# Holding a layer's projections close behind the attention that they are woven with, and moving one gate tile to another buffer tag

## The chip, the cores and the metric

The kernel runs on one core of one Trainium2 chip. The metric is the device time of one execution in microseconds. Before the change it is 1248.79 us, the median of three runs (1248.63 to 1249.88).

## The reference

Two transformer layers work on 512 latent tokens (an 8 x 64 grid) and 256 context tokens, D = 1024, heads of 64. Each layer computes, in float32:

```
hx = rmsnorm(x) * (1 + scale) + shift          # shift, scale, gate from c @ ada_w + ada_b
px = hx @ w_in                                 # 1024 x 4608, split into q, k, v of A, B, C and a gate path
ya = A: global attention, 8 heads, 2 kv heads, q and k normalised and rotated
yb = B: neighbourhood attention, 8 heads, 8 x 16 window, learned bias
yc = C: window of +-128 tokens, 8 heads, 2 kv heads, a sink logit
x  = x + gate * ((concat(ya, yb, yc) * silu(px_gate)) @ w_out)
```

All three kinds of attention also read the 256 context keys. In the first layer the context tokens are queries too and are carried on; in the second they are only keys. A final RMSNorm gives the output.

## The kernel before, in words

**Precision.** Every large product is taken in three: each operand is split into a high and a low float32r part (hi x hi, hi x lo, lo x hi). So a projection of one 512-column bank is 8 k-tiles x 3 = 24 matmuls, and each weight tile is split first, by ScalarE (line 172, the high part) and VectorE or GpSimd (line 175, the low part).

**Stages.** For each layer, `mixers` runs the projections and the attention, then a stage of eight output blocks (`block`) multiplies by `w_out`. In front of the first layer stands the normalisation of x.

**Projections.** `proj_f` (matmuls on line 237) gives features x tokens: one bank of 512 latent columns and, where the context is wanted, one of 256. `proj_t` (line 258) gives tokens x features: two token tiles to a bank, 48 matmuls of 256 columns. Both take PSUM banks of tag pj, of which there are two, and hand a finished bank to a callback `done`, traced at high priority. The callbacks split Q, K and V, rotate (A's pairs 1 to 3 on GpSimd, lines 576 to 657), and compute the gates: `g_silu` (lines 634 and 635) for A and B, `c_g` (lines 779 and 780) for C.

**Attention.** A *pair* is two heads of one kind: B0 to B3, A0 to A3, C0 to C3. For each unit of a pair `scores` multiplies Q and K (line 881 for A, 924 and 926 for C, 979 and 981 for B, 846 for the context queries) and takes maximum and exponential. `values` transposes the probabilities (lines 901, 953, 1006, 864), splits them (line 553 on ScalarE and 798 on VectorE) and multiplies by V (`pv`, line 804). The values of one unit are zipped with the scores of the next. `finish` divides by the sums, transposes the result (line 1070) and multiplies by the gate; for C that is on GpSimd (lines 1076 and 1078), and the last read of C's gate.

**The weave.** `PLAN` (line 32) lists steps. Each step runs one pair's attention and the projections for later pairs: A0 with C's k, v and pair c0; C0 with a1; A1 with c1; C1 with a2; A2 with c2; C2 with a3; A3 with c3. The four B steps carry B's remaining projections, A's k and v, and a0. `weave` (line 1129) draws from two generators in turn, so that both progress in the same share of their estimated TensorE time. The attention's estimates are 16.5 (A) and 12.5 (B, C), plus 2.7 in layer 0 (lines 1211 and 1212); each `yield` tells how much was just issued. C3, the last, is woven with `head`, which reloads the finished products u (tile uf) and starts the first two output blocks (line 426).

**What sets the order on an engine.** The weave gives only the order in which instructions are traced, and with it their priority. The framework then schedules them by a timeline that it estimates when the program is built (line 1369): on each engine it takes the ready instruction of the highest priority, so an instruction traced later may be placed earlier when those ahead of it are not ready. The order on each engine is fixed from then on. `after` (line 96) adds a dependency without a semaphore: an order on one engine, and no wait between engines.

**Buffers.** A tag is a set of equal rooms, and a tile waits until a room is free. Tag gt has three rooms of 768 columns: the gates of A, B and C, and the reloaded uf of the head (line 404). Tag bm has two of 1152 columns: B's bias masks, one for each head (line 1154), and C's mask msk of 896 columns (line 1172), which is loaded once per layer when A0 begins and read until C3's scores. The reloaded u are split into the h tiles that the projections have read.

Of the kernel before, what the change touches and what calls it, by code (L numbers as in the profile page):

```python
# [18 lines left out]
D = 1024  # L19
# [26 lines left out]

CFG = dict(hp=600, hpf=600, pj=2, T=2, O=1, P=5, qt=5, kt=4, vt=4, gt=3, wh=5, ws=3, pt=3, bm=2, tA=1, OT=1, u=1, tl=1, ab="pj", tR=1, map={}, ada=2, h0=300, h1=1000, a0=9, H=2, hr=0, cp="A", cv="A", w0="D", w1="D", w2=(("D", "D"), ("D", "D")), hb="D", ws_="P")

# [12 lines left out]
def body(tc, xT, small, bcast, rpb, adaw, wt, wf, wo, trigA, trigC, mskB, mskC, outT):  # L61
# [153 lines left out]
    def wrap_h(kt):  # L215
        for h in (hh, hl):
            t = h[kt][2]
            nc.scalar.activation(t[:, 0:64], t[:, NT:NT + 64].bitcast(F32), AF.Copy)

    def off_tile(h, t):  # L220

        return h[2][:, t * 128:t * 128 + 128] if t < 4 else cols(h, t * 128, 128)

    def proj_f(l, s, need_ctx, bank, done):

        banks = early.pop(("f", s), None)
        w = None if banks else load_wf(l, s)
        for c0, n in ((0, NT), (NT, NCX)):
            if c0 and not need_ctx:
                continue  # L230
            p = banks.pop(0) if banks else bank()
            i = 0
            for kt in range(KT if w else 0):
                wh, wl = w[kt // 4]
                r = kt % 4
                for a, b in ((wh, hh), (wh, hl), (wl, hh)):
                    nc.tensor.matmul(p[:, 0:n], a[:, r, :], cols(b[kt], c0, n), start=(i == 0), stop=(i == 23))  # L237
# [7 lines left out]
    def proj_t(l, s, tiles, bank, done, tok=None):  # L245

        tok = tok or (lambda h, t: cols(h, t * 128, 128))
        banks = early.pop(("t", s), None)
        w = None if banks else load_wt(l, s)
        for t2 in range(0, tiles, 2):  # L250
            p = banks.pop(0) if banks else bank()
            for t in range(0 if w is None else 2):
                i = 0
                for kt in range(KT):
                    wh, wl = w[kt // 2]
                    r = kt % 2
                    for a, b in ((hh, wh), (hh, wl), (hl, wh)):
                        nc.tensor.matmul(p[:, t * 256:(t + 1) * 256], tok(a[kt], t2 + t), b[:, r, :],  # L258
                                         start=(i == 0), stop=(i == 23))
# [267 lines left out]
def mixers(tc, nc, l, last, p1, ps, const, env):  # L527
    g_ = env
    en = g_["en"]
    (pj, Sbig, psT, psO, half_O, opv, after, ADA, wlo, proj_f, proj_t, ada, ada_load, ident, identr, bc, onesw, mhalf, negsink, udram, dram, hpool, rpb,  # L530
# [243 lines left out]
    def c_g(i, bank):  # L774
        G = newG()

# [16 lines left out]
    def pt_copy(T, n):  # L793
# [5 lines left out]
        return hi, lo  # L799

    def pv(O, v, pt, o, c0, n, first, final):

        for x in range(2):
            a = nc.tensor.matmul(O if c0 is None else O[:, c0:c0 + n], v, pt[x][:, o:o + n], start=first and x == 0,  # L804
                                 stop=final and x == 1, skip_group_check=True)
# [35 lines left out]
    class CtxUnit(Unit):  # L841
        def scores(self):
            S = Sbig[:, 0:512]
            for t in range(2):
                for x in range(2):
                    nc.tensor.matmul(S[:, t * 256:(t + 1) * 256], self.Q[:, NT + t * 128:NT + (t + 1) * 128],
                                     self.K[:, x, NT:NA], start=(t == 0 and x == 0), stop=(x == 1),
                                     skip_group_check=True)
# [11 lines left out]
        def values(self):  # L860
            T = psT()
            for kb in range(2):
                for t in range(2):
                    nc.tensor.transpose(T[:, (2 * kb + t) * 128:(2 * kb + t + 1) * 128],
                                        self.P[:, t * 256 + kb * 128:t * 256 + (kb + 1) * 128], ident)
# [8 lines left out]
    class GlobalUnit(Unit):  # L874
        def scores(self):
            self.P = []
            for i in self.tiles:
                cx, loc = ((512, 0), (768, 1024))[i % 2]
                for c0, c1, o in ((NT, NA, cx), (0, NT, loc)):
                    for x in range(2):  # L880
                        nc.tensor.matmul(Sbig[:, o:o + c1 - c0], self.Q[:, i * 128:(i + 1) * 128],  # L881
                                         self.K[:, x, c0:c1], start=(x == 0), stop=(x == 1), skip_group_check=True)
# [10 lines left out]
        def values(self):  # L893
            O = half_O()
            for k2 in range(0, 6, 2):
                T = psT()
                for k in range(2):
                    for j in range(2):

                        o = ((k2 + k + 2) % 6 if j else k2 + k) * 128  # L900
                        nc.tensor.transpose(T[:, (2 * k + j) * 128:(2 * k + j + 1) * 128], self.P[j][:, o:o + 128],  # L901
                                            ident)
# [9 lines left out]
    class BandUnit(Unit):  # L912
        def scores(self):
# [3 lines left out]
            for pair in ((1, 2), (0, 3)):  # L917
                for i in pair:
# [4 lines left out]
                    for x in range(2):  # L923
                        nc.tensor.matmul(Sbig[:, cx:cx + 256], q, self.K[:, x, NT:NA],
                                         start=(x == 0), stop=(x == 1), skip_group_check=True)
                        nc.tensor.matmul(Sbig[:, loc:loc + nl], q, self.K[:, x, ks[0] * 128:ks[0] * 128 + nl],  # L926
                                         start=(x == 0 and nl > 256), stop=(x == 1), skip_group_check=True)
# [18 lines left out]
        def values(self):  # L946
            O = psO()
            for n, kb in enumerate((4, 5, 0, 1, 2, 3)):
                qs = [i for i in range(4) if kb in self.pos[i]]
                T = psT()  # L950
                for j, i in enumerate(qs):
                    o = self.pos[i][kb]
                    nc.tensor.transpose(T[:, j * 128:(j + 1) * 128], self.P[i][:, o:o + 128], ident)  # L953
                k = len(qs) * 128
# [6 lines left out]
    class NearUnit(Unit):  # L961
# [9 lines left out]
        def scores(self):  # L971
            self.P = {}
            for i in (1, 2, 0, 3):
# [4 lines left out]
                for x in range(2):  # L978
                    a = nc.tensor.matmul(S[:, cx:cx + 256], q, self.K[:, x, NT:NA], start=(x == 0), stop=(x == 1),  # L979
                                         skip_group_check=True)  # L980
                    b = nc.tensor.matmul(S[:, loc:loc + nl], q, self.K[:, x, k0:k0 + nl], start=False,  # L981
                                         stop=(x == 1), skip_group_check=True)
# [16 lines left out]
        def values(self):  # L999
            O = psO()  # L1000
            for n, kb in enumerate((4, 5, 1, 2, 3, 0)):
                qs = [i for i in range(4) if kb in self.PLAN[i][4]]
                T = psT()
                for j, i in enumerate(qs):
                    o = self.PLAN[i][4][kb]
                    nc.tensor.transpose(T[:, j * 128:(j + 1) * 128], self.P[i][:, o:o + 128], ident)  # L1006
                k = len(qs) * 128
# [34 lines left out]
    def finish(c):  # L1042
# [22 lines left out]
        for c0, n in ((0, 4), (4, nq - 4)):  # L1065
# [3 lines left out]
            for t in range(n):  # L1069
                nc.tensor.transpose(T[:, t * 128:(t + 1) * 128],  # L1070
                                    R[:, c0 + t].rearrange("p h f -> p (h f)"), ident)
# [302 lines left out]
```

## Time and profile before

| what | us |
|---|---|
| median of three runs | 1248.79 |
| the profiled execution, its own time | 1248.77 |
| its span, from the first to the last instruction | 1247.0 |
| busy VectorE / ScalarE / GpSimd | 751.5 / 709.7 / 414.5 |

The profile is that of one execution. Busy time of TensorE is that of its matmuls, whose ends are modelled. A row "line engine op out<-in xcount: minimum/median/maximum, first to last" gives durations in ns and the first and last start in us from the span's start. A row of waits gives the waiting instruction, what it waited for, the total, the number and the longest, in us. A row of a stretch gives its bounds and length, each engine's busy time with its number of instructions, the granted TensorE clock, the share of time in which the DMA engines were busy, and GB/s.

In layer 0 the projections and attention run until about 634 us and in layer 1 from about 718 to 1187 us; output blocks follow each.

### The profile page before, as it was taken

The page shows a single profiled execution, that of the slowest core. Times are in us where ns is not written, and L with a number is a line of the kernel's source. Part 1 is how long each engine was busy: PE and PEld are TensorE (multiplying, and loading weights), DVE is VectorE, ACT ScalarE, POOL GpSimd, SP SyncE. Part 2 cuts the span into 40 slices and gives each one's busy share as a digit, 9 for nine tenths or more (in the row PEclk, how much of TensorE's full clock was granted, in tenths as well). Part 3 has the DMA queues.
Part 4 walks back from the last instruction along what each step waited for, and adds up shares of the span by engine and source line. Part 5 has one row for each costly group of instructions (what it writes and reads, how often), then busy time and mean ns, then how long its engine had stood idle before and what let it go on. Part 6 is the DMA issues. An engine that isn't in the chain of part 4 may idle for free.

```text
span 1247.0 us, 21968 instructions
## 1 busy us (share of the span) xinstructions
PE 1177.4 (94%) x8100; PEld 1044.2 (84%) x8100; DVE 751.5 (60%) x1541; ACT 709.7 (57%) x1606; POOL 414.5 (33%) x505
## 2 busy tenths in 40 slices
PE   5999999999999999998899999999999989898996
PEld 3899999898888888886778989989989979777874
DVE  5665666754656647557654864676653465667653
ACT  5454555665655556567644743555665665767651
POOL 2530211353454355534210020201363754634200
PEclk9999999999999999999899999999999999999997
DMA  9442222312244234112245642333222211111251
GB/s 333 158 133 76 91 78 89 113 60 89 86 130 142 81 127 132 47 43 72 77 161 168 187 146 76 94 93 101 87 72 71 70 51 52 43 51 35 85 160 68
DMA packets 59627, 125.55 MB, mean 101 GB/s; under 512 B 7168, under 2 KB 11392, under 8 KB 59520
## 3 DMA queue, kind: packets, MB, share of 16 engines
q1 hardware_dynamic: 53280, 112.48, 28.6%
q10 hardware_dynamic: 6240, 11.67, 2.7%
q8 instruction: 64, 1.05, 0.3%
q14 instruction: 43, 0.35, 0.1%
HBM read 111.41 MB, written 10.09 MB: 97 GB/s over the span
## 4 chain that ended last, share of the span: by engine, by line
PE 77%; DVE 7%; issue 6%; ACT 4%; POOL 2%; DMA 2%; ACTq 0%; SPq 0%; POOLq 0%; DVEq 0%
PE pj L237 18%; PE pj L258 17%; PE Obig L804 8%; PE pj L426 4%; PE Sbig L881 3%; PE T L901 3%; PE T L258 2%; PE Sbig L426 2%; PE T L1006 2%; PE T L953 2%; PE pj L139 2%; PE Sbig L339 1%; PE T L426 1%; PE Sbig L926 1%; PE Sbig L979 1%
## 5 line engine op out<-in xcount | busy, mean ns | idle before, releaser
L798 DVE TENSOR_TENSOR ptl<-T,pth 128x512 fp32r<-128x512 f32 (+2 forms) x312 | 179.6, 590 | 120.3 <-ACT pth L553 118.3
L553 ACT ACTIVATE pth<-T 128x512 fp32r<-128x512 f32 (+2 forms) x312 | 157.1, 519 | 134.9 <-PE T L1006 46.1
L172 ACT ACTIVATE wh<-ws 128x512 fp32r<-128x512 f32 x216 | 133.8, 628 | 116.2 <-PE pj L237 26.8
L258 PE MATMUL pj<-wh,hL 128*128 128x256 f32 x896 | 179.0, 288 | 1.1 <-DVE kt L681 0.9
L237 PE MATMUL pj<-hL,wh 128*128 128x512 f32 x544 | 175.4, 398 | 4.8 <-ACT wh L172 3.0
L804 PE MATMUL Obig<-pth,vt 128*128 128x256 f32 (+2 forms) x432 | 134.9, 321 | 14.3 <-ACT pth L553 8.1
L258 PEld LDWEIGHTS pj<-wh,hL 128*128 128x128 f32 x896 | 143.6, 191 | 5.0 <-issue 2.0
L175 DVE TENSOR_TENSOR wl<-ws,wh 128x512 fp32r<-128x512 f32 x140 | 101.0, 728 | 72.9 <-ACT wh L172 66.5
L804 PE MATMUL Obig<-ptl,vt 128*128 128x256 f32 (+2 forms) x432 | 133.3, 323 | 2.7 <-DVE ptl L798 2.0
L258 PE MATMUL pj<-wl,hL 128*128 128x256 f32 x448 | 128.7, 287 | 0.0
L175 POOL TENSOR_TENSOR wl<-ws,wh 128x512 fp32r<-128x512 f32 x76 | 98.4, 1305 | 89.2 <-ACT wh L172 79.9
L237 PEld LDWEIGHTS pj<-hL,wh 128*128 128x128 f32 x544 | 100.0, 190 | 23.9 <-ACT wh L172 3.5
L237 PE MATMUL pj<-hL,wl 128*128 128x512 f32 x272 | 107.9, 397 | 0.0
L804 PEld LDWEIGHTS Obig<-pth,vt 128*128 128x128 f32 x432 | 82.2, 190 | 26.5 <-ACT pth L553 17.7
L804 PEld LDWEIGHTS Obig<-ptl,vt 128*128 128x128 f32 x432 | 82.3, 191 | 11.9 <-DVE ptl L798 7.0
L1160 POOL TENSOR_TENSOR bm<-wr,bm 128x192 f32<-128x192 f32 (+1 forms) x48 | 38.0, 821 | 153.4 <-DMA bm<-mskB_dram 108.8
L258 PEld LDWEIGHTS pj<-wl,hL 128*128 128x128 f32 x448 | 85.5, 191 | 0.8 <-issue 0.4
L887 DVE TENSOR_REDUCE negm<-Sbig 128x1 f32<-128x768 f32 x64 | 61.0, 954 | 32.3 <-PE Sbig L881 18.6
L935 DVE CUSTOM_DVE_ANT_0 P<-Sbig,msk,negsink 128x640 f32<-128x640 f32 (+1 forms) x64 | 50.9, 815 | 38.6 <-PE Sbig L926 17.2
L815 DVE TENSOR_TENSOR OT<-Obig,otmp 64x512 f32<-64x512 f32 (+1 forms) x88 | 45.0, 511 | 41.2 <-ACT otmp L814 39.8
L237 PE MATMUL pj<-hC,wh 128*128 128x256 f32 x336 | 66.9, 288 | 0.7 <-DVE gt L780 0.5
L992 DVE CUSTOM_DVE_ANT_0 P<-Sbig,bm 128x512 f32<-128x512 f32 (+1 forms) x64 | 41.9, 655 | 41.5 <-PE Sbig L981 28.3
(297 smaller groups left out, 2949.7 us busy)
## 6 DMA issues: line engine op xcount, KB each, us to landing
ada<-adaw_dram SPq DMA_DIRECT2D x48, 512.0 KB, 4.6
ws<-wf_dram SPq DMA_DIRECT2D x72, 256.0 KB, 2.8
ws<-wt_dram SPq DMA_DIRECT2D x72, 256.0 KB, 3.0
ws<-wo_dram SPq DMA_DIRECT2D x72, 256.0 KB, 2.8
bm<-mskB_dram SPq DMA_DIRECT2D x16, 576.0 KB, 4.0
u<-u ACTq DMA_DIRECT2D x9, 384.0 KB, 2.9
uf<-u SPq DMA_DIRECT2D x9, 384.0 KB, 3.0
tB<-tA ACTq DMA_DIRECT2D x40, 64.0 KB, 2.4
```

The source lines that it names most:

```text
L172: nc.scalar.activation(hi, src, AF.Copy)
L175: eng.tensor_sub(lo, src, hi.bitcast(F32))
L237: nc.tensor.matmul(p[:, 0:n], a[:, r, :], cols(b[kt], c0, n), start=(i == 0), stop=(i == 23))
L258: nc.tensor.matmul(p[:, t * 256:(t + 1) * 256], tok(a[kt], t2 + t), b[:, r, :], start=(i == 0), stop=(i == 23))
L426: nc.tensor.matmul(p[:, 0:n], a[:, r, :], ucols(ua[b][ft], c0, n), start=(ft == FT_ORDER[0] and i == 0), stop=(ft == FT_ORDER[-1] and i == 2))
L553: nc.scalar.activation(out, src, AF.Copy)
L798: nc.vector.tensor_sub(lo[:, 0:n], T[:, 0:n], hi[:, 0:n].bitcast(F32))
L804: a = nc.tensor.matmul(O if c0 is None else O[:, c0:c0 + n], v, pt[x][:, o:o + n], start=first and x == 0, stop=final and x == 1, skip_gro ...
L815: nc.vector.tensor_add(OT[64 * h:64 * h + 64, c0:c0 + n], O[0:64, 0:n], tmp[:, 0:n])
L887: nc.vector.tensor_reduce(nm, S, axis=AX.X, op=OP.max, negate=True)
L935: nc.vector.tensor_tensor_reduce(out=P[:, 0:n], in0=Sbig[:, s0:s0 + n], in1=self.bm()(i), op0=OP.add, op1=OP.min, scale=-1.0, scalar=self. ...
L992: nc.vector.tensor_tensor_reduce(out=P[:, p0:p0 + n], in0=S[:, 0:n], in1=self.bm()(i), op0=OP.add, op1=OP.min, scale=-1.0, scalar=3.0e38, ...
```

## The change

Two things are done.

1. Every TensorE instruction of the attention (scores, transposes, products with V, transposes of `finish`) is issued by the helpers `mul` and `turn`, which note its name in `pace["pe"]`. `weave` keeps a list of the attention's progress xa with the latest such name. Before it draws from the projections, it sets `pace["at"]` to the newest one that lies at least `lead` = 6.0 units back, or to none. In `proj_f` and `proj_t` every third matmul (the first of each k-tile's three) is ordered on TensorE behind that instruction, by `after`. The list starts anew with each step, so that the first 6.0 units of a step set no order; the step without attention and the head have none either.
2. C's gate is no longer a tile of tag gt, but one of tag bm. The number and size of the rooms stay the same.

```
+    pace = {"at": None, "pe": None}
+
+    def paced(mm, i):
+        if i % 3 == 0 and pace["at"]:
+            after(mm, pace["at"])
...
-                    nc.tensor.matmul(p[:, 0:n], a[:, r, :], cols(b[kt], c0, n), start=(i == 0), stop=(i == 23))
+                    paced(nc.tensor.matmul(p[:, 0:n], a[:, r, :], cols(b[kt], c0, n), start=(i == 0),
+                                           stop=(i == 23)), i)
...
     def c_g(i, bank):
-        G = newG()
+        G = p1.tile([128, NA], F32, name="gc", tag="bm", bufs=CFG["bm"])
...
+    def mul(*args, **kw):
+        m = nc.tensor.matmul(*args, **kw)
+        pace["pe"] = m.ins.name
+        return m
...
         xa = xb = 0.0
         la = a is not None
+        past = []
+        pace["pe"] = None
         while True:
             if la and xa * tb <= xb * ta:
                 try:
                     xa += next(a)
+                    past.append((xa, pace["pe"]))
                 except StopIteration:
                     la = False
             else:
+                while len(past) > 1 and past[1][0] <= xa - CFG["lead"]:
+                    past.pop(0)
+                pace["at"] = past[0][1] if past and past[0][0] <= xa - CFG["lead"] else None
                 try:
                     xb += next(b)
                 except StopIteration as r:
+                    pace["at"] = None
```

`turn` is to `nc.tensor.transpose` what `mul` is to `nc.tensor.matmul`. `proj_t` has the same edit as `proj_f`, and the other lines of the diff put `mul` and `turn` in the place of the two calls.

More of the change, by code (lines that the diff above doesn't have):

```diff
@@ L45 @@
 RSPAN = 7 * 31 + 48
-CFG = dict(hp=600, hpf=600, pj=2, T=2, O=1, P=5, qt=5, kt=4, vt=4, gt=3, wh=5, ws=3, pt=3, bm=2, tA=1, OT=1, u=1, tl=1, ab="pj", tR=1, map={}, ada=2, h0=300, h1=1000, a0=9, H=2, hr=0, cp="A", cv="A", w0="D", w1="D", w2=(("D", "D"), ("D", "D")), hb="D", ws_="P")
+CFG = dict(lead=6.0, hp=600, hpf=600, pj=2, T=2, O=1, P=5, qt=5, kt=4, vt=4, gt=3, wh=5, ws=3, pt=3, bm=2, tA=1, OT=1, u=1, tl=1, ab="pj", tR=1, map={}, ada=2, h0=300, h1=1000, a0=9, H=2, hr=0, cp="A", cv="A", w0="D", w1="D", w2=(("D", "D"), ("D", "D")), hb="D", ws_="P")
 WT_A_KV, WT_A, WT_BV, WT_BG = 0, 1, 5, 7
@@ L257, in proj_t @@
                     for a, b in ((hh, wh), (hh, wl), (hl, wh)):
-                        nc.tensor.matmul(p[:, t * 256:(t + 1) * 256], tok(a[kt], t2 + t), b[:, r, :],
-                                         start=(i == 0), stop=(i == 23))
+                        paced(nc.tensor.matmul(p[:, t * 256:(t + 1) * 256], tok(a[kt], t2 + t), b[:, r, :],
+                                               start=(i == 0), stop=(i == 23)), i)
                         i += 1
@@ L528, in mixers @@
     g_ = env
-    en = g_["en"]
+    en, pace = g_["en"], g_["pace"]
     (pj, Sbig, psT, psO, half_O, opv, after, ADA, wlo, proj_f, proj_t, ada, ada_load, ident, identr, bc, onesw, mhalf, negsink, udram, dram, hpool, rpb,
@@ L799, in pt_copy, with turn @@
         return hi, lo
+    def mul(*args, **kw):
+        m = nc.tensor.matmul(*args, **kw)
+        pace["pe"] = m.ins.name
+        return m
+    def turn(*args, **kw):
+        m = nc.tensor.transpose(*args, **kw)
+        pace["pe"] = m.ins.name
+        return m
     def pv(O, v, pt, o, c0, n, first, final):
         for x in range(2):
-            a = nc.tensor.matmul(O if c0 is None else O[:, c0:c0 + n], v, pt[x][:, o:o + n], start=first and x == 0,
+            a = mul(O if c0 is None else O[:, c0:c0 + n], v, pt[x][:, o:o + n], start=first and x == 0,
                                  stop=final and x == 1, skip_group_check=True)
@@ L845, in scores @@
                 for x in range(2):
-                    nc.tensor.matmul(S[:, t * 256:(t + 1) * 256], self.Q[:, NT + t * 128:NT + (t + 1) * 128],
+                    mul(S[:, t * 256:(t + 1) * 256], self.Q[:, NT + t * 128:NT + (t + 1) * 128],
                                      self.K[:, x, NT:NA], start=(t == 0 and x == 0), stop=(x == 1),
@@ L863, in values @@
                 for t in range(2):
-                    nc.tensor.transpose(T[:, (2 * kb + t) * 128:(2 * kb + t + 1) * 128],
+                    turn(T[:, (2 * kb + t) * 128:(2 * kb + t + 1) * 128],
                                         self.P[:, t * 256 + kb * 128:t * 256 + (kb + 1) * 128], ident)
@@ L880, in scores @@
                     for x in range(2):
-                        nc.tensor.matmul(Sbig[:, o:o + c1 - c0], self.Q[:, i * 128:(i + 1) * 128],
+                        mul(Sbig[:, o:o + c1 - c0], self.Q[:, i * 128:(i + 1) * 128],
                                          self.K[:, x, c0:c1], start=(x == 0), stop=(x == 1), skip_group_check=True)
@@ L923, in scores @@
                     for x in range(2):
-                        nc.tensor.matmul(Sbig[:, cx:cx + 256], q, self.K[:, x, NT:NA],
+                        mul(Sbig[:, cx:cx + 256], q, self.K[:, x, NT:NA],
                                          start=(x == 0), stop=(x == 1), skip_group_check=True)
-                        nc.tensor.matmul(Sbig[:, loc:loc + nl], q, self.K[:, x, ks[0] * 128:ks[0] * 128 + nl],
+                        mul(Sbig[:, loc:loc + nl], q, self.K[:, x, ks[0] * 128:ks[0] * 128 + nl],
                                          start=(x == 0 and nl > 256), stop=(x == 1), skip_group_check=True)
@@ L952, in values @@
                     o = self.pos[i][kb]
-                    nc.tensor.transpose(T[:, j * 128:(j + 1) * 128], self.P[i][:, o:o + 128], ident)
+                    turn(T[:, j * 128:(j + 1) * 128], self.P[i][:, o:o + 128], ident)
                 k = len(qs) * 128
@@ L978, in scores @@
                 for x in range(2):
-                    a = nc.tensor.matmul(S[:, cx:cx + 256], q, self.K[:, x, NT:NA], start=(x == 0), stop=(x == 1),
+                    a = mul(S[:, cx:cx + 256], q, self.K[:, x, NT:NA], start=(x == 0), stop=(x == 1),
                                          skip_group_check=True)
-                    b = nc.tensor.matmul(S[:, loc:loc + nl], q, self.K[:, x, k0:k0 + nl], start=False,
+                    b = mul(S[:, loc:loc + nl], q, self.K[:, x, k0:k0 + nl], start=False,
                                          stop=(x == 1), skip_group_check=True)
@@ L1005, in values @@
                     o = self.PLAN[i][4][kb]
-                    nc.tensor.transpose(T[:, j * 128:(j + 1) * 128], self.P[i][:, o:o + 128], ident)
+                    turn(T[:, j * 128:(j + 1) * 128], self.P[i][:, o:o + 128], ident)
                 k = len(qs) * 128
@@ L1069, in finish @@
             for t in range(n):
-                nc.tensor.transpose(T[:, t * 128:(t + 1) * 128],
+                turn(T[:, t * 128:(t + 1) * 128],
                                     R[:, c0 + t].rearrange("p h f -> p (h f)"), ident)
```

2 lines of the change are left out of this document (1 added, 1 removed).

## The prediction

> **What bounds the kernel now.** I read the page's busy rows and slices first, then the busy time of stretches, then TensorE's waits in the worst stretch, then first and last starts of single lines.
>
> ```profile
> span 1247.0 us, 21968 instructions
> PE 1177.4 (94%) x8100; PEld 1044.2 (84%) x8100; DVE 751.5 (60%) x1541; ACT 709.7 (57%) x1606; POOL 414.5 (33%) x505
> PE   5999999999999999998899999999999989898996
> PEclk9999999999999999999899999999999999999997
> ```
>
> TensorE (PE) is the bound: 94% busy against 60% for the next engine. Idle is 1247.0 - 1177.4 = 69.6 us, and that is all that an edit which only reorders can win. The slices put it at the start, the end, and in two dips. By stretches, cut by the attention steps whose starts are shown further on:
>
> ```profile
> core 0: us, PE busy (x) PEld busy (x) DVE busy (x) ACT busy (x) POOL busy (x), PEclk, DMA share, GB/s
> ...
> 275.00:549.00 274.00, 268.68 (x2024) 233.13 (x2023) 157.07 (x350) 160.88 (x376) 127.64 (x149) 1.00 0.30 100
> 549.00:625.00 76.00, 63.51 (x365) 51.64 (x366) 54.19 (x93) 52.33 (x120) 29.32 (x34) 0.96 0.22 68
> ...
> 775.00:1001.00 226.00, 222.26 (x1593) 207.00 (x1592) 128.78 (x279) 128.21 (x294) 83.54 (x105) 1.00 0.28 82
> 1001.00:1150.00 149.00, 134.65 (x857) 116.90 (x856) 92.71 (x172) 103.34 (x229) 70.75 (x83) 0.98 0.15 45
> ...
> 1225.00:1247.00 22.00, 9.90 (x43) 7.90 (x41) 7.17 (x12) 2.31 (x4) 1.02 (x1) 0.71 0.25 95
> ```
>
> PE is full in 275 to 549 (5.32 us idle, 1.9%) and 775 to 1001 (3.74 us, 1.7%). At the end of each layer's attention it is not: 12.49 us idle in 549 to 625 (16.4%), 14.35 us in 1001 to 1150 (9.6%). The 12.10 us of the tail after 1225 aren't touched. In the first dip PE waits for the softmax chain, in small pieces:
>
> ```profile
> PE T L953 <- DVE ptl L798: 2.0, 3, 1.0
> PE Obig L804 <- ACT P L856: 1.4, 1, 1.4
> PE Obig L804 <- DVE OT L815: 1.4, 2, 0.8
> PE pj L426 <- ACT hL L398: 1.3, 2, 1.0
> ```
>
> Such waits cost nothing where other matmuls stand ready. Next, first scores of A1, C1, A2, C2, A3 and C3 in layer 0 (lines 881 and 924), and the last matmul of pair c3's projections, which are written to be woven with A3:
>
> ```profile
> L881 PE MATMUL Sbig<-kt,qt x32: 274/389/481, 369.5 to 406.7; 128*128 128x256 f32 x16, 128*128 128x512 f32 x16
> L924 PE MATMUL Sbig<-kt,qt x16: 277/282/365, 419.6 to 454.9; 128*128 128x256 f32 x16
> L881 PE MATMUL Sbig<-kt,qt x32: 274/378/398, 464.3 to 493.9; 128*128 128x256 f32 x16, 128*128 128x512 f32 x16
> L924 PE MATMUL Sbig<-kt,qt x16: 278/282/384, 506.9 to 541.6; 128*128 128x256 f32 x16
> L881 PE MATMUL Sbig<-kt,qt x32: 273/390/400, 549.4 to 576.5; 128*128 128x256 f32 x16, 128*128 128x512 f32 x16
> L924 PE MATMUL Sbig<-kt,qt x16: 278/288/562, 588.7 to 616.5; 128*128 128x256 f32 x16
> L237 PE MATMUL pj<-hC,wl x16: 280/283/284, 530.4 to 545.8; 128*128 128x256 f32 x16
> ```
>
> c3 is over at 545.8, before A3 begins at 549.4: projections have run a whole step ahead, and A3 and C3 have none left to fill their waits. Layer 1 is the same: c3's last start is 1100.5, A3's first score 1120.9.
>
> ```profile
> L237 PE MATMUL pj<-hL,wh x64: 388/390/481, 1024.0 to 1100.5; 128*128 128x512 f32 x64
> L881 PE MATMUL Sbig<-kt,qt x32: 275/394/629, 1120.9 to 1143.8; 128*128 128x256 f32 x16, 128*128 128x512 f32 x16
> ```
>
> **Part 1, the pace.** No instruction is added; it is an order on PE, so its own cost is 0. From 6.0 units of attention on, every third projection matmul stands behind the attention instruction 6.0 units back. In A3 of layer 0 a step has 16.5 + 2.7 = 19.2 units, so 6.0/19.2 = 31% of c3 is free and 69% goes behind A3's start. Prices of projections, from uninterrupted runs in the chain:
>
> ```profile
> 66.90 11.52 PE T L258 x96
> 84.66 5.47 PE pj L237 x24
> ```
>
> That is 0.228 us for a matmul of 512 columns, 0.120 for 256. c3 in layer 0 is two times (24 x 0.228 + 24 x 0.120): 16.7 us. So 0.69 x 16.7 = 11.5 us move behind 549, into 12.49 us of idle. If the idle falls to the 1.9% of the stretch before (1.5 us), 11.0 us are won. Can attention move up by that? A3, with no projection beside it, took 588.7 - 549.4 = 39.3 us; A2 took 42.6 and A1 50.1, so the A steps alone have 14.1 us of slack. C2 with 42.5 and C1 with 44.7 have nothing unloaded to compare with. Against it: DVE and ACT are busy 71% and 69% in the dip (54.19 and 52.33 of 76), which no order of PE shortens. I take half of 11.0: 5.5 us, ends 0 and 11.0.
>
> Layer 1 has no context queries: 64% of c3 (1 - 6.0/16.5, of 2 x 5.47 = 10.9 us), 7.0 us, moves into A3, and 52% of a3 (1 - 6.0/12.5, of 96 x 0.120 = 11.5 us), 6.0 us, into C2: 13.0 us against 14.35 us idle. At 1.7% residue (2.5 us) the most is 11.9. Here a second thing holds, which part 2 lifts, so I take 60%: 7.1 us.
>
> Who needs what is held back: the Q of the next pair. In layer 0 the GpSimd rotation of one bank ran, where nothing held it, from 492.5 to 498.0 + 0.74:
>
> ```profile
> L576 ACT ACTIVATE qs<-pj x1: 383/383/383, 492.5 to 492.5; 128x256 f32<-128x256 f32 x1
> L650 POOL TENSOR_TENSOR qd<-tC,qd x1: 735/735/735, 498.0 to 498.0; 128x256 fp32r<-128x256 f32 x1
> ```
>
> That is 6.2 us. The last paced matmul may stand at (15.2 - 6.0)/15.2 = 61% of a C step of 42 us, 16 us ahead of the next step: covered, price 0. Without that cover it would be 6.2 us a step.
>
> The head (the first two output blocks) can split reloaded u only once c3 has freed the h tiles. That will be later than 545.8, but the head didn't start then anyway:
>
> ```profile
> L1076 POOL TENSOR_TENSOR u<-OT,gt x1: 1540/1540/1540, 560.2 to 560.2; 128x512 f32<-128x512 f32 x1
> L406 SPq DMA_DIRECT2D uf<-u x8: 319/320/330, 563.7 to 599.7; - x8
> L426 PE MATMUL pj<-hL,wh x10: 389/397/501, 569.6 to 579.4; 128*128 128x512 f32 x10
> ```
>
> Reloads share tag gt with the gates. The first issues at 563.7, behind C2's finish (560.2 + 1.54), and eight take 36 us, 5.1 us each, for want of a second room. With C's gates elsewhere two rooms are open, and eight should take about half. If c3 ends near 575, the head ends about where it does now: price 0, ends -3 and +3. SP's queue then waits less in front of the output weights.
>
> **Part 2, the gate's room.** In layer 1 gates in gt stop the projections:
>
> ```profile
> L1076 POOL TENSOR_TENSOR u<-OT,gt x1: 1556/1556/1556, 1021.2 to 1021.2; 128x512 f32<-128x512 f32 x1
> L635 DVE SCALAR_TENSOR_TENSOR gt<-th,pj x2: 409/416/422, 1022.8 to 1024.3; 128x256 f32<-128x256 f32 x2
> L258 PE MATMUL pj<-wh,hL x64: 278/283/385, 981.5 to 1002.8; 128*128 128x256 f32 x64
> ```
>
> a2's matmuls end at 1002.8, its gate is written at 1022.8, the moment C0's finish (1021.2 + 1.56) gives a room back, and c2's projections begin at 1024.0: 21 us without a projection. Afterwards gt holds A's gates alone and this stop goes. What is late next: C's mask holds one of bm's two rooms, so gate c(i) waits for the finish of C(i-1). In layer 0 c3's gate was written from 541.6; it may not be before 561.8.
>
> ```profile
> L780 DVE SCALAR_TENSOR_TENSOR gt<-th,pj x2: 407/547/687, 541.6 to 547.8; 128x512 f32<-128x512 f32 x1, 128x256 f32<-128x256 f32 x1
> L779 ACT ACTIVATE th<-pj x12: 365/578/597, 313.0 to 1101.5; 128x512 f32<-128x512 f32 x8, 128x256 f32<-128x256 f32 x4
>   DVE gt L635: 1.5, 2
> ```
>
> Unpaced, its bank would stay taken 561.8 - 547.8 = 14.0 us. One of two pj banks is left, and tanh and gate (0.58 + 0.69 = 1.27 us) no longer overlap the next bank; 2 banks fit in 14 us, so up to 2.5 us a gate, six gates (c1 to c3, two layers), 15 us. On DVE the waiting gate has the softmax's subtractions (line 798) queued behind it; the same wait of A's gate for GpSimd cost 1.5 us in all (third line). But the pace puts the gate into the second half of the step, minus 31%, where C(i-1)'s finish is about over, and attention matmuls fill PE meanwhile. I take 0.5 us a gate, 3 us, ends 0 and 15. The Trainium skill (Perfetto Trace Analysis, Optimizing Tensor Performance, Matmuls) asks that groups rotate through banks so that one's evacuation overlaps the next; by that rule alone I would book the 15 us and end at 1251. No row of this trace shows a bank held so. The room in gt and the pace both shorten the hold, which is why I don't.
>
> **The sum.** 5.5 + 7.1 - 3.0 = 9.6 us less. The profiled execution took 1248.77 us, 1.77 beyond its span, as good as the median 1248.79; so about 1239.
>
> **Rivals.** *The whole dip is won*: 11.0 + 11.9 = 22.9 us, 1226. For it: the clock, 0.96 and 0.98 in the dips, would rise too. Against it: attention would have to follow without loss. By weight loads the room is larger: their share is 85% and 92% in the full stretches, so 51.64 and 116.90 us at those shares take 60.7 and 127.6 instead of 76 and 149, 36.7 us less, 1212. The Trainium skill (Perfetto Trace Analysis, Identifying the Most-Contended Engine) holds that share for the better measure of headroom; the trace agrees in so far as 84% stands beside the 94% of the matmuls. I give this end 0.04 of its own: attention has many transposes, and chain latency isn't PE's headroom.
>
> *Attention sets the pace*: its steps take about 40 us with or without projections (39.3 against 42.6 and 42.5), so held work only swaps idle now for idle later: 1248.8. The A1 step of 50.1 us and PE at 98% before the dip speak against.
>
> *Slower: held projections stand behind a waiting attention matmul.* PE takes its matmuls in the order written. Where filler was already through, it will be queued behind the wait. Place: the two full stretches, 500 us with 9.06 us idle (1.8%). Each percent more is 5.0 us; from 3.7% on the 9.6 us are gone. At 5%, a fifth of the way to the dip's 16.4%, it is 15.9 us more idle: 1255. The small total of waits there now speaks for it as much as against: that is what the lead buys.
>
> *It doesn't do what it says*: in B's steps 6.0/15.2 = 39% of each step is free and the lead may hardly shrink; that gives part of the forecast, and lies in it or in no change.
>
> **Numbers.** Forecast (1232 to 1246) 0.42; whole dip 0.12 and the end by weight loads 0.04; attention sets the pace 0.14; slower 0.28. A measurement here tells about 0.2%, 2.5 us, from no change. Faster 0.58, same 0.14, slower 0.28. The range 1225 to 1256 leaves out about 0.08 on each side; it holds the gate's 15 us (1251) and the queue at 5%. The forecast's own range is 1232 to 1246.
>
> **What will show it.** Right: c3's last projection stands well inside A3 (about two thirds through) in both layers; idle of the dips falls to about 7 and 7 us; the full stretches keep under 2.5%; in layer 1 no 20 us gap ahead of c2; reloads come at under 4 us each. Wrong: PE waits for L553 or L798 grow inside the full stretches; DVE idles ahead of line 780; A steps stay at 40 us while PE idles earlier; or c3 still ends before A3 starts.

## The result and the profile after

The changed kernel takes 1229.49 us (median of four runs, 1228.29 to 1232.05), the kernel before 1249.34 us beside it. The ratio is 0.9846 with a 95% interval of 0.9834 to 0.9857: 1.5% faster, some 19.8 us, where 9.8 us had been forecast (1248.79 to 1239). That is below the forecast's own range (1232 to 1246).

The page of the profiled execution (1228.29 us), same lines as before:

```profile
span 1226.5 us, 21963 instructions
PE 1172.5 (96%) x8100; PEld 1038.5 (85%) x8100; DVE 755.1 (62%) x1541; ACT 713.1 (58%) x1606; POOL 415.4 (34%) x505
PE   5999999999999999999899899999999999989996
PEclk9999999999999999999999999999999999999998
```

TensorE, VectorE, ScalarE and GpSimd have as many instructions as before (the counts behind the x), in another order. TensorE's idle time went from 69.6 to 54.0 us. That is 15.6 of the 20.5 us by which the span shrank; the other 4.9 us are busy time (1177.4 to 1172.5). The granted clock is 9 in every slice but the last, where before one slice in the first dip had 8 and the last 7; the mean went from 0.988 to 0.993, and 0.5% of 1177 us is 5.9 us. The last section shows what these means stand for.

The same stretches as in the prediction, laid so that the two dips end, or begin, at the same steps: A3 of layer 0 now begins at 534 instead of 549, and C3 of layer 1 at 1131 instead of 1150.

```profile
core 0: us, PE busy (x) PEld busy (x) DVE busy (x) ACT busy (x) POOL busy (x), PEclk, DMA share, GB/s
260.00:534.00 274.00, 271.32 (x2026) 232.77 (x2025) 165.54 (x364) 164.80 (x384) 129.46 (x156) 1.00 0.32 104
534.00:610.00 76.00, 71.05 (x432) 60.63 (x431) 52.36 (x91) 54.51 (x125) 38.10 (x40) 0.98 0.23 69
756.00:982.00 226.00, 222.64 (x1575) 204.73 (x1574) 141.82 (x297) 135.10 (x309) 81.19 (x104) 1.00 0.27 81
982.00:1131.00 149.00, 139.97 (x914) 122.57 (x913) 89.54 (x159) 102.78 (x222) 82.12 (x90) 1.00 0.22 64
1204.50:1226.50 22.00, 9.92 (x47) 7.77 (x45) 7.55 (x13) 2.71 (x4) 1.02 (x1) 0.76 0.25 95
```

Idle in the first dip fell from 12.49 to 4.95 us, in the second from 14.35 to 9.03; the full stretches stay full (2.68 and 3.36 us idle), and the tail is untouched (12.08). In the first dip TensorE now starts 432 matmuls in 76 us, where it started 365. What it still waits for there:

```profile
PE Sbig L811 <- DVE negm L954: 1.6, 2, 1.3
PE Obig L811 <- ACT pth L561: 1.3, 3, 0.7
PE Obig L811 <- DVE OT L834: 0.6, 1, 0.6
PE Sbig L811 <- ACT P L908: 0.5, 1, 0.5
```

No instruction of the softmax chain was taken away, but TensorE's waits for it are now mostly covered: the products with V (Obig) wait 1.3 us for ScalarE and 0.6 us for the output's sum, and the transposes' wait for VectorE's subtraction, 2.0 us before, is no longer in the list.

Where c3's projections of layer 0 stand (line 244 was 237), and where A3 and C3 begin (all scores are now recorded on line 811; A's have 512 columns, C's 384):

```profile
L244 PE MATMUL pj<-hC,wl x16: 279/283/415, 533.5 to 569.4; 128*128 128x256 f32 x16
L811 PE MATMUL Sbig<-kt,qt x42: 274/354/400, 533.6 to 579.9; 128*128 128x256 f32 x25, 128*128 128x512 f32 x16, 128*128 128x384 f32 x1
```

c3's last matmul starts at 569.4, 77% through A3 (533.6 to 579.9), instead of before it. In layer 1 c3 ends 69% through A3, which lasts from 1093.8 to C3's start at 1131.6 (the first of the 17 matmuls is still c2's):

```profile
L244 PE MATMUL pj<-hL,wl x17: 389/393/476, 1059.7 to 1119.8; 128*128 128x512 f32 x17
L811 PE MATMUL Sbig<-kt,qt x32: 274/388/400, 1093.8 to 1122.1; 128*128 128x256 f32 x16, 128*128 128x512 f32 x16
```

The gate and the head's reload in layer 0:

```profile
L1095 POOL TENSOR_TENSOR u<-OT,gc x1: 1577/1577/1577, 547.6 to 547.6; 128x512 f32<-128x512 f32 x1
L789 DVE SCALAR_TENSOR_TENSOR gc<-th,pj x2: 421/554/686, 563.8 to 572.9; 128x512 f32<-128x512 f32 x1, 128x256 f32<-128x256 f32 x1
L414 SPq DMA_DIRECT2D uf<-u x7: 319/326/327, 561.0 to 578.8; - x7
L434 PE MATMUL pj<-hL,wh x23: 387/393/481, 566.3 to 579.2; 128*128 128x512 f32 x23
```

C2's finish reads the old gate at 547.6, and c3's new one is written at 563.8: the held bank that the prediction booked with 3 us didn't occur. Nor does it elsewhere: in the whole trace line 789 waits for ScalarE alone, 1.5 us in all. The seven reloads shown come 3.0 us apart instead of 5.1; with the pace alone, the gate in gt, nine come 5.1 us apart (554.9 to 595.7).

For the runs below, one table by stages is of use. The marks are the first 512-column scores of A0, the first 384-column scores of C3 and the first 192-column scores of B0 (its third query tile), each taken from the trace; us, with TensorE's idle time in brackets:

| run | 75 to A0 | A0 to C3 | C3 to B0 of layer 1 | B0 to A0 | A0 to C3 | C3 to end | span |
|---|---|---|---|---|---|---|---|
| before | 194.8 (3.1) | 319.2 (12.4) | 190.8 (9.7) | 150.0 (2.0) | 220.7 (15.9) | 96.6 (12.9) | 1247.0 |
| after | 189.9 (0.6) | 315.0 (4.3) | 184.6 (8.0) | 142.4 (0.9) | 224.6 (11.5) | 94.9 (15.2) | 1226.5 |
| pace alone | 190.4 (0.6) | 311.3 (4.8) | 190.9 (8.4) | 142.4 (1.0) | 218.3 (12.7) | 104.4 (15.6) | 1232.8 |
| room alone | 195.4 (3.1) | 324.4 (11.4) | 181.6 (7.3) | 150.0 (2.0) | 232.3 (15.3) | 92.0 (15.9) | 1250.7 |
| lead 3 | 193.1 (3.3) | 315.1 (10.7) | 183.6 (11.7) | 149.7 (2.3) | 234.2 (16.7) | 96.1 (14.9) | 1246.9 |
| lead 12 | 194.4 (3.1) | 316.9 (6.4) | 181.0 (9.0) | 150.1 (2.0) | 236.9 (18.1) | 90.5 (15.0) | 1244.8 |

A stage gets shorter both by less idle time and by work that now stands behind its end, so the stages are to be read in sums. Layer 0 up to B0 of layer 1 gained 15.2 us, the rest 5.3 us. Each row is one execution: that of the change took 1.2 us less than its kernel's median, that of the pace alone (1234.58 us) 3.0 us more, so of the 6.3 us between these two spans 4.2 belong to the executions and not to the kernels.

### The profile page after: what moved, and what is told of

Its sections match the earlier page's. It is cut to its first block, busy times and chain, and to the rows that moved or that the text cites. A ratio compares the mean times of both kernels' runs of the same rounds, so it can differ in the third digit from the quotient of the medians.

```text
span 1226.5 us, 21963 instructions
## 1 busy us (share of the span) xinstructions
PE 1172.5 (96%) x8100; PEld 1038.5 (85%) x8100; DVE 755.1 (62%) x1541; ACT 713.1 (58%) x1606; POOL 415.4 (34%) x505
## 4 chain that ended last, share of the span: by engine, by line
PE 79%; issue 6%; DVE 5%; ACT 4%; DMA 2%; POOL 2%; ACTq 0%; POOLq 0%; SPq 0%; DVEq 0%
PE pj L244 19%; PE pj L266 17%; PE Sbig L811 9%; PE Obig L811 9%; PE T L816 8%; PE pj L434 4%; PE T L266 2%; PE Sbig L434 2%; PE pj L139 2%; PE Sbig L347 1%; PE T L434 1%; DVE ptl L807 1%; PE pj L347 1%; ACT wh L172 1%; PE Sbig L266 1%
## 5 line engine op out<-in xcount | busy, mean ns | idle before, releaser
L244 PE MATMUL pj<-hL,wh 128*128 128x512 f32 x544 | 178.7, 405 | 4.1 <-ACT wh L172 3.7
L816 PE MATMUL T<-ident,P 128*128 128x128 f32 x1024 | 167.3, 274 | 3.7 <-DVE ptl L807 1.8
L811 PE MATMUL Sbig<-kt,qt 128*128 128x256 f32 (+1 forms) x864 | 158.0, 309 | 2.2 <-DVE negm L954 1.6
L175 POOL TENSOR_TENSOR wl<-ws,wh 128x512 fp32r<-128x512 f32 x76 | 98.6, 1302 | 144.1 <-ACT wh L172 141.7
L816 PEld LDWEIGHTS T<-ident,P 128*128 128x128 f32 x1024 | 123.4, 140 | 18.7 <-DVE ptl L807 3.1
L811 PEld LDWEIGHTS Sbig<-kt,qt 128*128 128x128 f32 x864 | 124.8, 189 | 10.7 <-DVE negm L954 2.9
L244 PEld LDWEIGHTS pj<-hL,wh 128*128 128x128 f32 x544 | 96.8, 190 | 21.0 <-ACT wh L172 4.0
L906 DVE TENSOR_REDUCE negm<-Sbig 128x1 f32<-128x768 f32 x64 | 61.1, 954 | 39.3 <-PE Sbig L811 19.7
```

Source lines behind the costliest of these rows:

```text
L175: eng.tensor_sub(lo, src, hi.bitcast(F32))
L244: paced(nc.tensor.matmul(p[:, 0:n], a[:, r, :], cols(b[kt], c0, n), start=(i == 0), stop=(i == 23)), i)
L811: m = nc.tensor.matmul(*args, **kw)
L816: m = nc.tensor.transpose(*args, **kw)
L906: nc.vector.tensor_reduce(nm, S, axis=AX.X, op=OP.max, negate=True)
```

## Theories and experiments

Theory 1: filler that is held back for the ends of the layers makes the gain, and both parts are needed for it. Theory 2: the gate's room alone does it. Theory 3: any other order would have done, and the amount of lead doesn't matter. Ratios are to the kernel before, beside the same runs, with 95% intervals.

### The two parts by themselves

Pace alone:

```
-        G = p1.tile([128, NA], F32, name="gc", tag="bm", bufs=CFG["bm"])
+        G = newG()
```

> The pace alone, C's gate back in tag gt. Theory 1 (both parts work: the pace keeps filler for the ends of the layers, the room lifts the 21 us stop of the projections in layer 1): layer 0 as after the change, layer 1 part of the way back, 1233 to 1238 us. Theory 2 (the room alone does it: earlier reloads and no stop): 1244 us or more. Theory 3 (any other order would have done, the amount of lead doesn't matter): about 1230 us.

Measured: 1231.54 us, 0.9851 (0.9832 to 0.9871). Faster than theory 1 had it (1233 to 1238), and not to be told from the full change. So the gain doesn't need both parts; that half of theory 1 falls.

Room alone:

```
-        if i % 3 == 0 and pace["at"]:
+        if False:
```

> The gate's room alone, no order on the projections. Theory 1: the projections still run a step ahead, c3 is over before A3 begins in layer 0, and the dip of TensorE at the end of layer 0 stays; only the stop in layer 1 goes: 1242 to 1249 us. Theory 2: 1228 to 1234 us. Theory 3: within 5 us of 1230.

Measured: 1250.60 us, 1.0014 (1.0003 to 1.0025). Theory 2 falls: the room alone wins nothing. Theory 1 had the time within 2 us. In layer 0 c3's latent matmuls are over at 548.1, before A3 (from 550.5), as it said; but the last of its context matmuls stand at 561.4 to 565.0, while c3's first gate waits for its room (its tanh is at 548.5, its gate at 566.5). The idle time of A0 to C3 stays: 11.4 us, 12.4 before.

What the room does, the traces show in layer 1. Before the change a2's gate had to wait for a room in gt. The row below, of the kernel before, gives its tanh at 996.8; the gate's row in the prediction gives 1022.8. So one of the two projection banks was taken for 26 us, and a3's tanh waited as long, from 1056.6 to 1082.4.

```profile
L634 ACT ACTIVATE th<-pj x2: 365/372/378, 996.8 to 1023.6; 128x256 f32<-128x256 f32 x2
```

With the room alone A's gates are free of that wait, and C's have it: c1's tanh is at 975.6, and its gate is written at 1018.1, when C0's finish has read the old one (1016.6 + 1.54).

```profile
L788 ACT ACTIVATE th<-pj x1: 581/581/581, 975.6 to 975.6; 128x512 f32<-128x512 f32 x1
L1095 POOL TENSOR_TENSOR u<-OT,gc x1: 1535/1535/1535, 1016.6 to 1016.6; 128x512 f32<-128x512 f32 x1
L789 DVE SCALAR_TENSOR_TENSOR gc<-th,pj x1: 687/687/687, 1018.1 to 1018.1; 128x512 f32<-128x512 f32 x1
L266 PE MATMUL pj<-wh,hL x64: 277/283/364, 978.0 to 1032.1; 128*128 128x256 f32 x64
```

For 42.5 us one of the two projection banks is taken, and a2 needs 54 us (978.0 to 1032.1) instead of 21. The room doesn't do away with the stop; without the pace it puts another in its place. In the table it wins 9.2 us behind C3 of layer 0 (190.8 to 181.6), where the head's reload runs, and 4.6 us at the end, and loses 5.2 and 11.6 us while attention runs; all of it together costs 0.14%. The Trainium skill (Perfetto Trace Analysis, Optimizing Tensor Performance, Matmuls) asks that independent matmul groups rotate through different PSUM banks, so that one group's evacuation overlaps the next group's matmuls. The trace agrees: with one bank kept for 42.5 us, a2 took 54 us instead of 21.

With the pace no gate waits, yet the table has the same signs: 6.3 us less behind C3 and 9.5 us less at the end, against 3.7 and 6.3 us more under attention. That sums to 5.8 us, but 4.2 us of the difference belong to the executions, so no single stage of these two rows is sure. The head starts at 1098.9 instead of 1127.0 in layer 1, first after the change, then with the pace alone:

```profile
L434 PE MATMUL pj<-hL,wh x25: 387/395/505, 1098.9 to 1129.3; 128*128 128x512 f32 x25
```

```profile
L434 PE MATMUL pj<-hL,wh x22: 389/397/506, 1127.0 to 1149.5; 128*128 128x512 f32 x22
```

### Another lead

Two kernels with `lead=3.0` and `lead=12.0` in the table of constants.

> Both parts, with a lead of 3.0 units instead of 6.0. Theory 1: the projections stand a little later still, 1225 to 1232 us, and c3 ends at least 3 us later against A3. The rival on the slower side (held matmuls stand behind waiting attention) expects idle TensorE inside the steps and 1234 us or more. Theory 3: about 1230 us.

Measured: 1248.04 us, 0.9989 (0.9978 to 0.9999). The rival's side, and far beyond its threshold: the whole gain is gone. Three stages of this run (75 to A0 and C3 to B0 of layer 1, then A0 to C3 of layer 1), and the same three after the change:

```profile
75.00:268.10 193.10, 189.79 (x1421) 178.82 (x1421) 127.69 (x279) 108.53 (x271) 40.60 (x70) 1.00 0.26 80
583.20:766.80 183.60, 171.89 (x1062) 151.81 (x1061) 109.86 (x202) 95.03 (x201) 26.18 (x29) 0.98 0.44 136
916.50:1150.70 234.20, 217.52 (x1414) 194.05 (x1413) 130.52 (x232) 153.58 (x330) 124.97 (x139) 0.97 0.20 60
```

```profile
75.00:264.90 189.90, 189.33 (x1423) 179.63 (x1423) 126.17 (x279) 109.61 (x271) 37.76 (x70) 1.00 0.26 81
579.90:764.50 184.60, 176.59 (x1102) 157.19 (x1101) 112.37 (x208) 97.34 (x203) 22.64 (x30) 0.99 0.42 131
906.90:1131.60 224.70, 213.24 (x1395) 187.28 (x1394) 130.98 (x234) 153.11 (x329) 124.46 (x138) 1.00 0.21 63
```

With lead 3.0 TensorE idles 3.31, 11.71 and 16.68 us there, against 0.57, 8.01 and 11.46; and the second stage, with a length about the same, holds 40 matmuls fewer, which have to be done later.

> Both parts, with a lead of 12.0 units. Theory 1: most of the free run is back (in a C step of 15.2 units only the last fifth is held), so about half of the gain goes: 1236 to 1244 us, and c3 in layer 0 ends earlier against A3 than with 6.0. Theory 2 and 3: 1228 to 1232 us, as with 6.0.

Measured: 1247.04 us, 0.9984 (0.9968 to 1.0000). Slower than any theory expected. By the table it is two things: layer 0 up to B0 of layer 1 keeps 12.3 us of gain (767.4 instead of 779.7), and from there to the end the run takes 477.4 us, where the kernel before took 467.3 and the room alone 474.3. In layer 1 a B or C step has 12.5 units, so a lead of 12.0 holds next to nothing there. The held gate explains a part at most: C's gates do wait for their room, but c1's only from its tanh at 1002.6 to 1010.5, against 42.5 us with the room alone. Of the 10.1 us over the kernel before, 5.8 are busy time of TensorE (442.3 against 436.4 us) at a lower mean clock (0.97 against 0.98); where the rest comes from stays open. Theory 3 falls with these two runs: the lead decides between all and nothing.

### Pace in part

No pace in B's steps, and pace in layer 0 alone. `weave` takes `pace["lead"]` in place of `CFG["lead"]`, set ahead of each step (99.0 is more than a step has):

```
+        pace["lead"] = 99.0 if pair and pair[0] == "B" else 6.0
```

> Both parts, but no pace in the four B steps of a layer (lead 99 there). Theory 1 (what counts is filler for the last steps of a layer): B's steps as long as before the change (195 and 150 us) with more projections done in them, and the later steps that much shorter, so that most of the gain stays: 1229 to 1236 us. Rival (the B steps' own 5 and 8 us are a gain by themselves): 1240 to 1244 us.

Measured: 1236.03 us, 0.9892 (0.9876 to 0.9908). At the edge of theory 1: the B steps' pace is worth 6.5 us, a third of the gain. Theory 1 had B's steps at 195 and 150 us; they took 195.0 and 144.1. Between the two profiled executions 8.9 us of TensorE's idle time differ: 3.8 in the B steps themselves (3.1 and 2.2 us without their pace, 0.6 and 0.9 with it) and 5.1 in the stages behind them. That those had less filler left is the likely reason, not a shown one.

```
+        pace["lead"] = 99.0 if last else 6.0
```

> Both parts, but the pace only in layer 0; C's gate in bm in both layers. Theory 1 (without the pace the gate's room holds one of two projection banks, as in the run with the room alone, where layer 1 from B0 to the end took 474 us against 467 before): layer 0 as after the change, layer 1 as with the room alone, 1236 to 1241 us. Rival (the room costs nothing by itself and layer 1 gained little): 1229 to 1234 us.

Measured: 1242.87 us, 0.9961 (0.9949 to 0.9973), 1.9 us over theory 1's range. B0 of layer 1 begins at 765.4, as after the change (764.5), and from there the trace counts 474.9 us, the 474.3 us of the room alone. Here too c1's gate of layer 1 is held, from its tanh at 964.6 to 1007.2:

```profile
L788 ACT ACTIVATE th<-pj x1: 578/578/578, 964.6 to 964.6; 128x512 f32<-128x512 f32 x1
L789 DVE SCALAR_TENSOR_TENSOR gc<-th,pj x1: 686/686/686, 1007.2 to 1007.2; 128x512 f32<-128x512 f32 x1
```

So where the pace is missing in layer 1, the gate's room costs it 7 to 8 us there (474.9 and 474.3 against 467.3): here 4.1 us of busy time and 3.5 us of idle time.

### Why a lead of 3 loses

With lead 3.0 TensorE waits for GpSimd at the transposes of A's Q (line 662), which it doesn't after the change:

```profile
PE T L662 <- POOL qd L658: 9.5, 3, 3.3
```

Theory 1b took this for the cause: A's projections, woven with C's steps, come so late that the rotation's 6.2 us aren't covered any more. Three runs with lead 3.0 in one kind of step each, 6.0 elsewhere, as in:

```
+        pace["lead"] = 3.0 if pair and pair[0] == "A" else 6.0
```

> Both parts, lead 3.0 only in the A steps, which carry C's projections, and 6.0 in the C and B steps, which carry A's. Theory 1b (lead 3.0 everywhere lost the gain because A's Q, which GpSimd rotates, came late: TensorE waited 9.5 us on line 662): without that wait the gain is back, 1226 to 1234 us. Rival (held matmuls stand behind waiting attention whichever projections they are): 1238 us or more.

Measured: 1227.91 us, 0.9825 (0.9809 to 0.9842): no loss in the steps that carry C's projections. That is theory 1b's range, but it doesn't show its cause: the two runs below do.

> Both parts, lead 3.0 only in the C steps, which carry A's projections, 6.0 elsewhere. Theory 1b (with lead 3.0 everywhere it was A's Q that came late, out of GpSimd's rotation): TensorE waits again for GpSimd at the transposes of A's Q, 7 to 10 us in layer 1, and the time is 1236 to 1242 us. Rival (the B steps lost it: at a layer's start too little is free of the pace while B0's softmax starts up): 1227 to 1232 us and no such wait.

Measured: 1236.14 us, 0.9902 (0.9882 to 0.9922). A loss of 6.7 us against the change as it is, at the edge of theory 1b's range, but without the wait that was to make it; line 662 has this left:

```profile
PE T L662 <- POOL qd L658: 0.7, 1, 0.7
```

The rival's 1227 to 1232 missed as well.

> Both parts, lead 3.0 only in the B steps, 6.0 elsewhere. Theory 1b: 1228 to 1232 us. Rival (the start of a layer): 1236 to 1246 us, and less of b1's and v's projections done when B0 of layer 1 begins. If both hold a part, each of this run and the one before lies in between, 1232 to 1238 us.

Measured: 1238.91 us, 0.9932 (0.9910 to 0.9953). The rival's range: the B steps lose more, 9.4 us. The 18 us in which B0 of layer 1 starts, up to its third query tile, first after the change, then in this run:

```profile
747.00:765.00 18.00, 17.99 (x118) 16.36 (x117) 10.13 (x18) 8.85 (x18) 0.00 (x0) 1.00 0.27 88
```

```profile
745.00:763.00 18.00, 16.09 (x111) 14.15 (x111) 6.75 (x15) 6.58 (x14) 0.00 (x0) 1.00 0.22 75
```

Little of b1 is free of the pace, and between B0's first scores TensorE waits for VectorE's maxima; the row has these waits from 755 to 765 us. After the change there are none in that stretch, and b1's matmuls stand between the scores.

```profile
PE Sbig L811 <- DVE negm L1011: 1.4, 2, 0.8
```

TensorE idles 1.91 us instead of 0.01. v1 of layer 1 begins 14.4 us later, while B0's first scores come 1.6 us later (758.7 instead of 757.1) and its third tile 2.1 us earlier; the first row is after the change, the second this run:

```profile
L266 PE MATMUL pj<-wh,hL x64: 278/283/365, 765.4 to 780.6; 128*128 128x256 f32 x64
```

```profile
L266 PE MATMUL pj<-wh,hL x64: 278/283/387, 779.8 to 795.0; 128*128 128x256 f32 x64
```

So theory 1b is wrong as the cause: none of the three runs has the wait for GpSimd in any size, only the one that is short of lead everywhere. By the medians, losses of 6.7 and 9.4 us and a gain of 1.6 make 14.5 us, of 18.6 us with lead 3.0 everywhere. What makes the 6.7 us in the C steps stays open; the traces only say where it lies: in layer 1 TensorE idles 8.1 us in A0, A1 and A2 with lead 3.0 in the C steps, and 3.1 us after the change, while C0, C1 and C2 idle 4.1 and 5.4 us.

### The head's reload apart from the gate

If the room pays through the head's reload and costs through a held bank, the reload can have the room instead of the gate: C's gate back in gt, and uf in bm, where C's mask leaves one free.

```
-        uf = pool.tile([128, NA], F32, name="uf", tag="gt", bufs=CFG["gt"])
+        uf = pool.tile([128, NA], F32, name="uf", tag="bm", bufs=CFG["bm"])
```

> Pace as changed, C's gate back in gt, and the head's reloaded uf in tag bm instead, beside C's mask. Theory 1a (the gate's room pays only because it frees gt for the head's reload, and costs a held bank while attention runs): attention stages as short as with the pace alone (A0 to C3 311 and 218 us), output stages as short as with both (185 and 95 us), in all 1217 to 1224 us. Rival (the room helps the gates themselves): no better than the pace alone, 1229 to 1235 us.

Measured: 1227.94 us, 0.9822 (0.9802 to 0.9842). Between the two ranges. Layer 0 keeps the short attention (312.4 us), but the stage behind it takes 187.4 us, and in layer 1 the attention is as long as after the change (224.5 us). There the head begins at 1101.2:

```profile
L434 PE MATMUL pj<-hL,wh x28: 389/395/635, 1101.2 to 1138.3; 128*128 128x512 f32 x28
```

No gate of C can wait for bm here, and the stage is long all the same. So the longer attention stage of layer 1 isn't the held bank's doing: more of the head's work lies within it (1379 matmuls start there in this run and 1395 after the change, 1354 with the pace alone). The two sums, to the end from A0, are 321.0 us here, 319.6 after the change and 322.7 with the pace alone.

With two rooms, `room = ("bm", "gt")[j % 2]` for reload j:

> As the one before, but the reloaded uf alternate between bm and gt, so that two are on their way once C2's gate is free. Theory 1a: as good or up to 3 us better, 1215 to 1224 us. Rival: 1229 to 1235 us.

Measured: 1228.61 us, 0.9833 (0.9816 to 0.9851). No further gain.

Lastly both single edits that stood at 1227.9 us, uf in bm with the gate in gt, and lead 3.0 in the A steps:

> The pace with lead 3.0 in the A steps and 6.0 elsewhere, C's gate back in gt, the head's uf in bm. If the two single edits (1227.9 us each) add up: 1224 to 1227 us. If they took the same idle time: 1227 to 1230 us.

Measured: 1226.43 us, 0.9827 (0.9808 to 0.9846), in the range of "they add up". It is the lowest median, but its interval overlaps that of the change (0.9834 to 0.9857), so it can't be said to be faster.

## Why the prediction was right, and where it was off

**The whole: right in mechanism and direction, half the size.** The sum gave 9.6 us, and 19.8 were measured, below the forecast's own range; only the wide range (1225 to 1256), which was there for the rivals, holds it. By TensorE's idle time in the table, the terms missed on both sides. Layer 0's attention gave up 8.1 us (5.5 booked). Layer 1's attention and the stage behind it gave up 2.1 us together (7.1 booked), and the held gates (3.0 booked as a cost) didn't occur. The B steps gave up 3.6 us and the stage behind C3 of layer 0 1.7 us, and busy time fell by 4.9 us; all three were booked at nothing. That layer 1's term was too high while these were left out is luck: with layer 1 sized right the forecast would have lain farther off.

**What bounds the kernel: right, with one sentence wrong.** TensorE's idle time at the ends of the layers was what could be won. c3 moved into A3 in both layers, the idle time of the dips fell to 4.95 and 9.03 us (about 7 and 7 had been named), and the full stretches stayed under 2.5% idle. But the 69.6 us of idle time are not "all that an edit which only reorders can win": 4.9 of the 20.5 us are busy time.

**Pace in layer 0: 5.5 us booked, mis-sized.** By the pace alone B0 of layer 1 begins 12.0 us earlier (767.7 against 779.7). Of that, 7.6 us are idle time of A0 to C3, the stage that holds most of the dip, so halving the 11.0 us for chain latency took off too much; in the dip itself idle time fell by 7.5 us with the full change. Another 2.5 us are idle time of the B steps, which the sum left out, and 1.3 us lie behind C3. The attention didn't merely follow: the steps evened out. By their first scores A1, A2 and A3 now take 46.2, 46.1 and 46.0 us (50.1, 42.6 and 39.3 before), and C1 and C2 38.2 and 37.0 us instead of 44.7 and 42.5. I had nothing unloaded to compare the C steps with, and they had the slack.

**Pace in layer 1: 7.1 us booked, too much.** With the pace alone, layer 1 from B0 to the end takes 465.1 instead of 467.3 us: 2.2 us, in an execution 3.0 us over its median, so hardly more than 5. With the full change it is 5.3 us. The dip's idle time did fall there (14.35 to 9.03 us), but the stage behind it, C3 to the end, has 2.3 us more.

**The clock** stood only in a rival, as a thing that would rise too, and the sum left it at 0. It rose. TensorE ran at half clock for about 17 us in all before the change, the tail apart, and for about 7 us after it; half of the difference is 5 us (an estimate), and busy time fell by 4.9. Executions of one kernel say the same: of the 40 of the kernel before that stand beside the experiments, the nine with a mean clock of 0.991 took 1245.17 to 1248.38 us, the three with 0.985 took 1251.15 to 1251.97. No run sets the clock by itself, so the clock as cause of the 4.9 us is well supported, but not isolated.

**The gate's room: 3.0 us of cost, ends 0 and 15.** In the changed kernel no gate is held, and the room is worth about 2 us (1231.54 to 1229.49), within the intervals. "No row of this trace shows a bank held so" was a misreading: the prediction's own row of line 635 is one, a2's gate, whose bank was taken for 26 us. That the room lifts layer 1's 21 us stop was wrong too: with the pace alone and the gate in gt, c2's projections (first row) start before a2's (second row) have ended, so the pace lifts it. Without the pace the room only moves the held bank from A's gates to C's.

```profile
L244 PE MATMUL pj<-hL,wh x18: 389/390/477, 1011.1 to 1040.6; 128*128 128x512 f32 x18
L266 PE MATMUL pj<-wh,hL x64: 276/283/384, 983.0 to 1030.4; 128*128 128x256 f32 x64
```

**Cover for A's Q: right at lead 6**, where line 662 isn't among TensorE's waits. With lead 3.0 the wait appears, 3.3 us at the longest against the 6.2 us that the prediction named for a step without cover.

**The head: price 0, ends -3 and +3.** Reloads come at 3.0 us, under the 4 us named. What the head is worth by itself isn't shown: the runs that move the reload (1227.94 and 1228.61 us) can't be told from the change.

**The rivals.** *Attention sets the pace* falls: from A1 to C3 of layer 0 the steps take 213.5 instead of 219.2 us, the C steps shorter, A2 and A3 longer. *Slower, held projections behind waiting attention* is a true mechanism with a point nearer than I had put it: at lead 3.0 idle time is 59.6 us over the six stages of the table against 40.5, and the gain is gone. The chance of 0.28 was for the edit as it stands, at 6.0. *The whole dip*, 1226, is about as near to the measured time as the forecast's range (3.5 and 2.5 us off), and from the runs with other rooms and leads, 1226 to 1229, there seems little more to take this way. By weight loads 1212 had been worked out: their share rose to 80% and 82% in the dips (from 68% and 78%), not to the 85% and 92% of the full stretches. The Trainium skill (Perfetto Trace Analysis, Identifying the Most-Contended Engine) holds the load share for the better measure of headroom. This case doesn't bear that out for a new order: by the load share 36.7 us were to be won, by the idle time of the dips 22.9, and the change won 19.8.

## What to carry to other kernels

Filler that has run ahead is lost where it is needed: look whether the work woven with a latency-bound chain ends before the chain does, and if so tie it behind the chain in the engine's order. The distance matters much (here 3 and 12 units both lost nearly all that 6 won), so it is tried by kind of step, with free filler left for the first step of a stage. When a tile is moved to a fuller tag, ask which PSUM bank is held while it waits.

## What the runs showed of the hardware

A mean clock a little under 1 is here a short time at half clock. The first dip's mean of 0.96 before the change comes of 6.8 us at 0.50. The rows give the 3.4 us ahead of it, the 6.8 us themselves and the 3.4 us behind it:

```profile
595.90:599.30 3.40, 1.85 (x11) 1.06 (x9) 2.15 (x4) 1.93 (x6) 1.23 (x1) 1.00 0.55 177
599.40:606.20 6.80, 5.98 (x21) 5.17 (x21) 3.75 (x7) 3.88 (x10) 4.11 (x3) 0.50 0.38 116
606.30:609.70 3.40, 3.40 (x21) 2.89 (x20) 1.23 (x2) 1.35 (x3) 0.94 (x1) 1.00 0.02 5
```

A 512-column matmul of line 426 lasts 0.63 us at 601.21 and 0.39 us at 606.96. Three more such stretches of about 3.4 us begin at 718.7, 1080.6 and 1135.2. In the 3.4 us ahead of these four TensorE was busy for 1.85, 0.35, 1.18 and 1.39 us, though in the dips no wait just there was longer than 1.75 us. After the change two are left besides the tail, from 703.8 and, in the first dip, from 540.0; ahead of the latter TensorE was busy for 2.42 of 3.4 us:

```profile
536.60:540.00 3.40, 2.42 (x11) 1.27 (x9) 2.05 (x5) 2.73 (x7) 1.84 (x3) 1.00 0.22 50
540.10:543.40 3.30, 3.30 (x16) 3.24 (x17) 0.86 (x2) 2.35 (x6) 0.50 (x1) 0.50 0.00 0
```

In the second dip, with its gaps in part filled, no half-clock stretch is left. The busy time, which holds this, is about a quarter of the gain (4.9 of 20.5 us). From which share of gaps on the clock halves, no run here tells.
